# Squares of the first blocks added on VectorE, and the entry's steps in another order

## The chip, the core and the metric

The kernel runs on one core of a Trainium2 chip, as one program. The time is that of one execution on the device, in microseconds (us). The core's engines are TensorE (PE; its weight loads are shown as PEld), VectorE (DVE), ScalarE (ACT), GpSimd (POOL) and SyncE (SP, which here only issues transfers). Each engine works through a queue of its own in order; semaphores tie the queues together.

## What is computed

The reference runs two layers of a streaming encoder over 1024 prompt tokens and 8 x 16 later tokens (together 1152) of width 1024. What matters here is the way into layer 0: each token is divided by the root of its mean square and multiplied by a gain, and one input projection follows, whose columns feed an attention branch and a recurrent branch.

```python
def rms_norm(x, g):
    y = xf * lax.rsqrt(jnp.mean(xf * xf, axis=-1, keepdims=True) + EPS)
    return (y * g.astype(jnp.float32)).astype(x.dtype)
...
h = x @ w_in            # q, k, v, xr (recurrent input), gr (its gate branch)
...
xc, new_buf = causal_conv(xr, conv_buf, conv_w, conv_b)
hs, new_h = rg_lru(xc, h0, wa, ba, wx, bx, lam)
rec = hs * jax.nn.gelu(gr)
```

The recurrence runs h = a h + b along the tokens, with a and b from two sigmoid gates that are products of the convolved input.

## The kernel before, in words

Activations lie transposed: width on the partitions, in 8 tiles of 128 (kt), tokens along the free axis, in three blocks (nb) of 384. Products are made in three passes of a split format: each operand is a high part (hi) and a low part (lo = value - hi), and `three` (L530 to L533) multiplies hi by hi (L531), hi by lo (L532) and lo by hi (L533). So a slab of one 128-column chunk over one block is 8 x 3 = 24 matmuls into one PSUM bank.

The norm's root is left out of the products' operands: a tile is only multiplied by its gain and split (`norm_split`: high part on ScalarE at L527, low part on VectorE at L528), and the root is multiplied in when the product is read from PSUM (`xr_evac`, L679 and L681; for the gate branch L696). The root itself takes these steps for a block:

- `stat` squares a tile (on ScalarE at L478; tile 4 on VectorE at L476) into one of three buffers `tmp`, and adds the square to the block's sum `s`, at L480: on GpSimd, unless `sum_on_dve` is set. At the entry it isn't.
- `stat_tokens`: three small matmuls with a column of ones (L490) give each token's sum; VectorE forms the root `rT` by a chain of small steps (L492, L452 to L457), each of which needs the one before.
- `spread_stat`: three small matmuls (L500) spread `rT` over the partitions; VectorE copies the result to `rstd` (L501).

The entry's order is written by hand in the string `START` (L263 to L265), which a loop (L713) walks. Its words: `w` splits half a weight slab (ScalarE L200, VectorE L201), `nBK` splits tile K of block B, `sBK` squares it and adds, `mCB` makes the slab of recurrent chunk C over block B, `fB` is `stat_tokens`, `FB` `spread_stat`, `eCB` evacuates the slab. Chunks 0 and 1 are made there for all three blocks; chunk 2's slabs follow. The order of issue gives instructions their rank; a scheduler then puts each engine's queue in order from it and from the tiles' dependences.

Behind the entry comes the recurrence stage (chunks c = 0 to 3): convolution (ScalarE L575, VectorE L578), split (L586, L590), gates (products, sigmoids at L613), tanh, exponent and root (L624, L627, L630) on ScalarE, VectorE L636 and L639, GpSimd L633, the scan L649 on VectorE, and then the next chunk's gates. The gate branch's slabs are made beside it, evacuated at L696 and put through GeLU at L700. ScalarE loads a table when it changes between sigmoid, exponent, root and GeLU. After it come attention and the MLPs, which are products for most of the span.

Of the kernel before, what the change touches and what calls it, by code (L numbers as in the profile page):

```python
# [248 lines left out]
class InOrder:  # L249
# [5 lines left out]
    def __getattr__(self, name):  # L255
# [5 lines left out]
ON_DVE = (4,)  # L261
WLOAD = {0: 1, 2: 2}
START = ("n00 w n03 w n01 w s00 n02 w n11 n04 s01 n07 n06 n17 s02 n05 m00 n12 n13 s03 n10 s04 m10 n14 n15 s05 n16 "  # L263
         "n25 s06 s07 m11 f0 n27 m01 s10 n21 s11 s12 n23 s13 n20 s14 s15 s20 s16 n26 n22 F0 s21 n24 m02 e00 m12 s22 s23 "
         "s17 e10 s24 s25 f1 s26 s27 F1 e01 e11 f2 F2 e02 e12")  # L265

LRU_ORDER = [(t[0], int(t[1])) for t in "x2 x2 x2 x3 G0 g0 x3 G1 g0 x3 G2 g0 g1 g1 g1 g2 g2 g2 G3 g3 g3 g3".split()]

# [13 lines left out]
def body(ctx, tc, io):  # L282
# [41 lines left out]
    def bank(tag):  # L324
        bank.n += 1
        p = banks[tag if tag in ("mm", "two") else "ax"].pool
        return p.tile([P, 1024 if tag == "two" else 512], F32, tag=tag, bufs=BANKS[tag], name=f"{tag}{bank.n}")
# [3 lines left out]
    def tmp():  # L331
        tmp.n += 1
        return space["st"].pool.tile([P, NBW], F32, tag="tmp", bufs=3, name=f"tmp{tmp.n}")
# [65 lines left out]
    def pump(act, dve, pl, halves=1):  # L399
        W.pump(halves)  # L400
        bg.pump(act, dve, pl)
# [62 lines left out]
    def stat(nb, kt, src, on_dve=False, sum_on_dve=False):  # L464
        if kt == 0:
            if nb == NB - 1 and "early" in space:
                s = space["early"].pool.tile([P, NBW], F32, tag="xc", bufs=2, name=f"s{stat.n}")
            else:
                s = space["st"].pool.tile([P, NBW], F32, tag="s", bufs=space["sums"], name=f"s{stat.n}")
            stat.n += 1  # L470
            ssum[nb] = s
            sq = s
        else:
            sq = tmp()
        if on_dve:
            nc.vector.tensor_mul(sq, src, src)  # L476
        else:
            nc.scalar.square(sq, src)  # L478
        if kt:
            (nc.vector if sum_on_dve else nc.gpsimd).tensor_add(ssum[nb], ssum[nb], sq)  # L480
# [3 lines left out]
    def stat_tokens(nb, tag="ax"):  # L484

        s = ssum.pop(nb)
        ps = bank(tag)
        n = NBW // P
        for t in range(n):
            nc.tensor.matmul(ps[:, t:t + 1], s[:, t * P:t * P + P], ones, start=True, stop=True)  # L490
        v, w, r = ps[:, 8:8 + n], ps[:, 16:16 + n], rT[:, nb * n:nb * n + n]
        nc.vector.tensor_scalar(v, ps[:, 0:n], 1.0 / D, EPS, OP.mult, OP.add)  # L492
        rsqrt(r, v, w)

    def spread_stat(nb, tag="ax"):
        n = NBW // P
        r = rT[:, nb * n:nb * n + n]
        ps = bank(tag)
        for t in range(n):
            nc.tensor.matmul(ps[:, t * P:t * P + P], r[:, t:t + 1].to_broadcast([P, P]), ident, start=True, stop=True)  # L500
        nc.vector.tensor_copy(rstd[:, nb * NBW:nb * NBW + NBW], ps[:, :NBW])  # L501
# [22 lines left out]
    def norm_split(nb, kt, src, gi):  # L524
        cols = slice(nb * NBW, nb * NBW + NBW)
        g = gt[:, gi, kt:kt + 1]
        nc.scalar.activation(xh[:, kt, cols], src, AF.Copy, scale=g)  # L527
        nc.vector.scalar_tensor_tensor(xl[:, kt, cols], src, g, xh[:, kt, cols].bitcast(F32), OP.mult, OP.subtract)  # L528
# [6 lines left out]
    def slab_bank(key, nb, kts=None, ps=None):  # L535

        h, l = W.get(key)
        cols = slice(nb * NBW, nb * NBW + NBW)
        if ps is None:
            ps = bank("mm")  # L540
        for kt in (kts or range(KT)):
            w = slice(kt * P, kt * P + P)
            three(ps[:, :NBW], h[:, w], l[:, w], xh[:, kt, cols], xl[:, kt, cols], kt == 0, kt == KT - 1)
        return ps
# [126 lines left out]
    def xr_evac(c, nb, ps):  # L671
        if nb == 0:
            t = pads[c] = xp.tile([P, PADW], F32, tag="xa", bufs=4, name=f"pad{c}")
            nc.gpsimd.memset(t[:, 0:3], 0.0)
            nc.gpsimd.tensor_scalar_mul(t[:, S0:].rearrange("p (b w) -> p b w", w=SW)[:, :, 0:3],
                                        lc[:, c, 16:40].rearrange("p (b w) -> p b w", w=3), 1.0)
        t = pads[c]
        n = min(NBW, SEQ - nb * NBW)
        nc.vector.tensor_mul(t[:, 3 + nb * NBW:3 + nb * NBW + n], ps[:, :n], rstd[:, nb * NBW:nb * NBW + n])  # L679
        if n < NBW:  # L680
            nc.vector.tensor_mul(  # L681
                t[:, S0:].rearrange("p (b w) -> p b w", w=SW)[:, :, 3:],
                ps[:, n:NBW].rearrange("p (b w) -> p b w", w=DS),
                rstd[:, SEQ:].rearrange("p (b w) -> p b w", w=DS))
            W.free(("xr", c))
            if c == 0:
                add_conv(0)
# [21 lines left out]
    def x_block(nb, kt):  # L709
        return xs[kt][:, nb * NBW:nb * NBW + NBW]  # L710

    early = {}
    for step in START.split():  # L713
        kind, *n = step[0], *(int(d) for d in step[1:])
        if kind == "w":
            W.split()
        elif kind == "n":
            norm_split(n[0], n[1], x_block(*n), 0)
        elif kind == "s":
            stat(n[0], n[1], x_block(*n), n[1] in ON_DVE)  # L720
        elif kind == "f":
            stat_tokens(n[0])
        elif kind == "F":
            spread_stat(n[0])
        elif kind == "m":
            c, nb = n
            early[c, nb] = slab_bank(("xr", c), nb, ps=bank("mm" if len(early) < 3 else "ax"))
        elif kind == "e":
            xr_evac(*n, early.pop(tuple(n)))
            pump(3200, 2500, 3000, 2)  # L730
# [1044 lines left out]
def build(arrays):  # L1775
    import concourse.bacc as bacc

    nc = bacc.Bacc("TRN2", target_bir_lowering=False, num_devices=1)
    io = {k: nc.dram_tensor(f"in_{k}", v.shape, F32, kind="ExternalInput").ap() for k, v in arrays.items()}
    for k, s in OUTS.items():  # L1780
        io[k] = nc.dram_tensor(f"out_{k}", s, F32, kind="ExternalOutput").ap()
    with tile.TileContext(nc) as tc, ExitStack() as ctx:
        body(ctx, tc, io)
    return nc
# [21 lines left out]
```

## Time and profile before

| | us |
|---|---|
| median of three runs (lowest, highest) | 2216.12 (2213.75, 2217.06) |
| the profiled execution | 2215.67 |
| its span | 2213.9 |
| TensorE busy | 2157.8 |
| VectorE busy | 1614.8 |
| ScalarE busy | 961.8 |
| GpSimd busy | 279.4 |

A timeline's row has the start, the duration, the engine, the line, the instruction, its output and inputs by the program's names, the shape, a count where rows were merged and, in brackets, how long the engine stood idle before it and what released it. Starts can lie closer together than durations are long, since instructions overlap at their ends; the distance of two starts is then the price in a full queue. A row of the waits has the total, the number and the longest. A row of the stretches has, for each engine, the busy time and the number of instructions, then the granted clock of TensorE (1.00 is full), the busy share of the DMA engines and GB/s.

### The profile page before, as it was taken

How to read it: one execution, taken by the hardware profiler on the slowest of the kernel's cores; microseconds unless marked ns; L12 is line 12 of the kernel's file. 1: busy time of each engine (PE TensorE's matmuls, PEld its weight loads, DVE VectorE, ACT ScalarE, POOL GpSimd, SP SyncE). 2: the span in 40 equal slices, each digit the busy share in tenths (PEclk: the TensorE clock that was granted, in tenths of full speed). 3: DMA queues.
4: the chain of work that ended last, by engine and by line, in shares of the span. 5: the costliest groups of instructions: out<-in, count | busy, mean ns of one | idle time of the engine just before them, and what ended most of it. 6: DMA issues, size and time to landing. Idle time of an engine off the chain costs nothing.

```text
span 2213.9 us, 37892 instructions
## 1 busy us (share of the span) xinstructions
PE 2157.8 (97%) x14980; PEld 2114.9 (96%) x14980; DVE 1614.8 (73%) x2810; ACT 961.8 (43%) x1695; POOL 279.4 (13%) x332
## 2 busy tenths in 40 slices
PE   7989999899999999999999999989999999999999
PEld 7978989899999999999988899989999999999999
DVE  8778883798777678777793734269877777877776
ACT  5665663367666642112162123226766665211211
POOL 5147642000000000000050333100000000000000
PEclk9999999999999999999999999999999999999999
DMA  4110043237666777356751013322766667735574
GB/s 156 63 51 9 13 142 103 67 124 278 241 224 243 264 297 291 102 188 248 254 181 50 20 48 109 113 75 94 292 240 231 234 250 308 282 128 205 209 249 149
DMA packets 108003, 377.91 MB, mean 171 GB/s; under 512 B 13473, under 2 KB 24737, under 8 KB 107809
## 3 DMA queue, kind: packets, MB, share of 16 engines
q1 hardware_dynamic: 107680, 375.47, 47.1%
q8 instruction: 118, 1.93, 0.4%
q14 instruction: 61, 0.49, 0.1%
q10 hardware_dynamic: 144, 0.02, 0.0%
HBM read 240.09 MB, written 136.26 MB: 170 GB/s over the span
## 4 chain that ended last, share of the span: by engine, by line
PE 88%; DVE 6%; ACT 2%; issue 2%; DMA 1%; POOL 1%; SPq 0%; ACTq 0%; DVEq 0%; POOLq 0%
PE two L1293 64%; PE mm L533 5%; PE mm L531 5%; PE mm L532 5%; PE mm L257 2%; PE mm L1610 1%; PE mm L1612 1%; PE mm L1611 1%; DVE w L201 1%; PE pv L257 1%; PE tp L257 1%; PE ax L1639 1%; PE qk L257 1%; DVE b L407 0%; DVE x L1492 0%
## 5 line engine op out<-in xcount | busy, mean ns | idle before, releaser
L1293 PE MATMUL two<-b,w 128*128 128x288 f32 x5424 | 728.0, 296 | 12.4 <-DVE x L1137 12.4
L1293 PEld LDWEIGHTS two<-b,w 128*128 128x128 f32 x5424 | 726.7, 189 | 12.9 <-ACT tmp L478 12.9
L1293 PE MATMUL two<-h,w 128*128 128x288 f32 x4704 | 630.6, 295 | 3.2 <-DVE x L1492 1.5
L1293 PEld LDWEIGHTS two<-h,w 128*128 128x128 f32 x4704 | 627.5, 188 | 5.1 <-issue 3.0
L200 ACT CAST w<-raw 128x512 fp32r<-128x512 f32 x542 | 331.2, 620 | 645.9 <-PE two L1293 412.7
L201 DVE TENSOR_TENSOR w<-raw,w 128x512 fp32r<-128x512 f32 x542 | 386.4, 718 | 113.7 <-ACT w L200 111.5
L1492 DVE TENSOR_TENSOR x<-two,x 128x576 f32<-128x576 f32 x448 | 336.3, 754 | 127.9 <-PE two L1293 126.4
L531 PE MATMUL mm<-xn0h,w 128*128 128x384 f32 x372 | 127.8, 343 | 6.3 <-ACT xn0h L527 5.9
L532 PE MATMUL mm<-xn1l,w 128*128 128x384 f32 x372 | 125.6, 338 | 1.1 <-DVE xn1l L528 1.1
L533 PE MATMUL mm<-xn0h,w 128*128 128x384 f32 x372 | 126.3, 340 | 0.0
L532 PE MATMUL mm<-xn0l,w 128*128 128x384 f32 x372 | 126.3, 340 | 0.0
L531 PE MATMUL mm<-xn1h,w 128*128 128x384 f32 x372 | 125.9, 339 | 0.0
L533 PE MATMUL mm<-xn1h,w 128*128 128x384 f32 x372 | 125.7, 338 | 0.0
L1542 POOL TENSOR_TENSOR s<-s,tmp 128x384 f32<-128x384 f32 (+1 forms) x28 | 28.9, 1059 | 730.7 <-ACT tmp L1541 730.6
L1293 PE MATMUL two<-hk,w 128*128 128x288 f32 x672 | 91.2, 295 | 0.0
L407 DVE TENSOR_TENSOR ho<-c_a,ho 128x576 fp32r<-128x576 f32 x78 | 57.2, 753 | 46.1 <-ACT ho L406 46.0
L1293 PEld LDWEIGHTS two<-hk,w 128*128 128x128 f32 x672 | 90.1, 188 | 0.0
L1322 ACT ACTIVATE c_a<-c_a 128x1152 f32<-128x1152 f32 x60 | 70.1, 1168 | 19.3 <-DVE c_a L1404 18.0
L531 PEld LDWEIGHTS mm<-xn0h,w 128*128 128x128 f32 x372 | 71.0, 191 | 7.3 <-ACT xn0h L527 6.6
L407 DVE TENSOR_TENSOR ho<-c_b,ho 128x576 fp32r<-128x576 f32 x96 | 72.3, 753 | 2.5 <-ACT ho L406 2.5
L480 POOL TENSOR_TENSOR s<-s,tmp 128x384 f32<-128x384 f32 x49 | 54.7, 1121 | 148.2 <-ACT tmp L478 146.0
L1137 DVE TENSOR_TENSOR x<-mm,x 128x384 f32<-128x384 f32 x48 | 26.7, 555 | 63.8 <-PE mm L533 63.6
(287 smaller groups left out, 2815.3 us busy)
## 6 DMA issues: line engine op xcount, KB each, us to landing
hidden<-ho SPq DMA_DIRECT2D x196, 576.0 KB, 4.0
h<-hidden SPq DMA_DIRECT2D x196, 576.0 KB, 6.6
raw<-in_w SPq DMA_DIRECT2D x136, 512.0 KB, 4.5
x<-scratch SPq DMA_DIRECT2D x24, 576.0 KB, 7.7
scratch<-x SPq DMA_DIRECT2D x48, 192.0 KB, 1.8
raw<-in_wo SPq DMA_DIRECT2D x16, 512.0 KB, 3.6
xin<-in_xT SPq DMA_DIRECT2D x24, 192.0 KB, 4.2
x<-in_xT SPq DMA_DIRECT2D x8, 576.0 KB, 3.8
```

Of the source, the lines that this page charges most:

```text
L200: nc.scalar.copy(t[:, 0], src)
L201: nc.vector.tensor_sub(t[:, 1], src, t[:, 0].bitcast(F32))
L257: return lambda *a, **k: self.tc.keep_in_program_order(op(*a, **k))
L407: nc.vector.tensor_sub(lo, src, hi.bitcast(F32))
L480: (nc.vector if sum_on_dve else nc.gpsimd).tensor_add(ssum[nb], ssum[nb], sq)
L531: nc.tensor.matmul(ps, wh, ah, start=start, stop=False)
L532: nc.tensor.matmul(ps, wh, al, start=False, stop=False)
L533: nc.tensor.matmul(ps, wl, ah, start=False, stop=stop)
L1293: nc.tensor.matmul(o, w, a[:, c], start=first and k == 0 and i == 0, stop=k == len(pairs) - 1 and i == 2, skip_group_check=True)
L1322: nc.scalar.activation(o, o, AF.Relu) if fn == "relu" else nc.scalar.square(o, o)
L1492: nc.vector.tensor_add(o, both(ps), o)
L1542: nc.gpsimd.tensor_add(o, o, sq)
```

## The change

All additions of squares at the entry go to VectorE, for all three blocks (21 instructions, tiles 1 to 7 of each). And `START` has another order from its 35th word on: block 2's tiles are split before any square of block 1 or 2 is taken, chunk 0's slab over block 2 (`m02`) stands ahead of block 0's spreading (`F0`), and the squares of blocks 1 and 2 come later, block 2's after the whole of block 1's.

```diff
 START = ("n00 w n03 w n01 w s00 n02 w n11 n04 s01 n07 n06 n17 s02 n05 m00 n12 n13 s03 n10 s04 m10 n14 n15 s05 n16 "
-         "n25 s06 s07 m11 f0 n27 m01 s10 n21 s11 s12 n23 s13 n20 s14 s15 s20 s16 n26 n22 F0 s21 n24 m02 e00 m12 s22 s23 "
-         "s17 e10 s24 s25 f1 s26 s27 F1 e01 e11 f2 F2 e02 e12")
+         "n25 s06 s07 m11 f0 n27 m01 n21 n23 n20 n26 n22 n24 m02 F0 s10 s11 e00 s12 m12 s13 s14 s15 s16 e10 s17 f1 "
+         "s20 s21 s22 s23 F1 e01 e11 s24 s25 s26 s27 f2 F2 e02 e12")
...
-            stat(n[0], n[1], x_block(*n), n[1] in ON_DVE)
+            stat(n[0], n[1], x_block(*n), n[1] in ON_DVE, True)
```

What becomes of it in the queues is shown at three places. In the rows, `ax` and `mm` are PSUM banks (the number tells one from another), `w` split weights, `xn0h` and `xn1h` the high parts of tiles 0 to 3 and 4 to 7, `xn0l` and `xn1l` the low parts, `xin` the unsplit tiles, `s` a block's sum.

TensorE around block 0's spreading, before:

```order
L532 MATMUL ax_319<-xn1l_84,w_160 128x384
L533 MATMUL ax_319<-xn1h_83,w_160 128x384
L500 MATMUL ax_376<-ident,rT 128x128 x3
L531 MATMUL ax_386<-xn0h_78,w_155 128x384
L532 MATMUL ax_386<-xn0l_79,w_155 128x384
```

TensorE at the same place now, from the end of chunk 0's slab over block 1 (ax_319):

```order
L533 MATMUL ax_319<-xn1h_83,w_160 128x384
L531 MATMUL ax_356<-xn0h_78,w_155 128x384
L532 MATMUL ax_356<-xn0l_79,w_155 128x384
...
L533 MATMUL ax_356<-xn1h_83,w_160 128x384
L500 MATMUL ax_381<-ident,rT 128x128 x3
L531 MATMUL ax_406<-xn0h_78,w_167 128x384
```

The 24 products of chunk 0 over block 2 (ax_386 before, ax_356 now) stand ahead of the spreading. In the same way, the last spreading has 16 more products ahead of it than before.

VectorE around block 0's root, before:

```order
L492 TENSOR_SCALAR ax_301<-ax_301 128x3
L555 TENSOR_SCALAR small<-lc 128x4
L452 TENSOR_SCALAR ax_301<-ax_301 128x3
L556 TENSOR_TENSOR small<-small,lc 128x4
L528 SCALAR_TENSOR_TENSOR xn1l_84<-xin_102,gt,xn1h_83 128x384
L453 TENSOR_SCALAR rT<-ax_301 128x3
L528 SCALAR_TENSOR_TENSOR xn0l_79<-xin_98,gt,xn0h_78 128x384
L455 SCALAR_TENSOR_TENSOR ax_301<-rT,ax_301 128x3
L476 TENSOR_TENSOR tmp_361<-xin_99 128x384
L456 TENSOR_TENSOR ax_301<-ax_301,rT 128x3
```

VectorE there now:

```order
L528 SCALAR_TENSOR_TENSOR xn1l_84<-xin_100,gt,xn1h_83 128x384
L480 TENSOR_TENSOR s_170<-s_170,tmp_273 128x384
L528 SCALAR_TENSOR_TENSOR xn0l_79<-xin_98,gt,xn0h_78 128x384
L492 TENSOR_SCALAR ax_301<-ax_301 128x3
L528 SCALAR_TENSOR_TENSOR xn1l_84<-xin_102,gt,xn1h_83 128x384
L452 TENSOR_SCALAR ax_301<-ax_301 128x3
L528 SCALAR_TENSOR_TENSOR xn0l_79<-xin_95,gt,xn0h_78 128x384
L453 TENSOR_SCALAR rT<-ax_301 128x3
L528 SCALAR_TENSOR_TENSOR xn1l_84<-xin_101,gt,xn1h_83 128x384
L455 SCALAR_TENSOR_TENSOR ax_301<-rT,ax_301 128x3
```

The last addition of block 0 (L480) is now in this queue, block 2's splits lie between the root's steps, and the preparation of the recurrence's constants (L555, L556) has gone further back.

ScalarE in the recurrence stage, between the second scan and the third, before (`u_1057` is chunk 1's gate branch, `rg` the gates, `h_983` chunk 2's recurrence):

```order
L613 ACT_TABLE_LOAD
L613 ACTIVATE rg_943<-ax_944,lc 128x392
...
L624 ACTIVATE h_983<-rg_943,spc 128x1176
L700 ACT_TABLE_LOAD
L700 ACTIVATE u_1057<-u_1057 128x1152
L627 ACT_TABLE_LOAD
L627 ACTIVATE rg_943<-rg_943,spc 128x1176
```

ScalarE there now:

```order
L700 ACTIVATE u_1057<-u_1057 128x1152
L613 ACT_TABLE_LOAD
L613 ACTIVATE rg_943<-ax_944,lc 128x392
...
L624 ACTIVATE h_983<-rg_943,spc 128x1176
L200 CAST w_1271<-raw_1045 128x512
L627 ACT_TABLE_LOAD
L627 ACTIVATE rg_943<-rg_943,spc 128x1176
```

The GeLU of chunk 1 went ahead of the gates, one table load is gone, and a weight cast stands in the GeLU's place. On VectorE, a gate-branch evacuation (L696) that stood ahead of the third scan stands behind it, and chunk 1's last one stands ahead of the second scan.

## The prediction

> **What bounds the kernel now.** I read the page's busy times first, then TensorE's waits up to 160 us, a table of stretches, and then the timelines of TensorE, VectorE and ScalarE.
>
> ```profile
> PE 2157.8 (97%) x14980; PEld 2114.9 (96%) x14980; DVE 1614.8 (73%) x2810; ACT 961.8 (43%) x1695; POOL 279.4 (13%) x332
> ...
> PE ax L500 <- DVE rT L457: 6.2, 2, 5.0
> ...
> PE mm L532 <- DVE xn1l L528: 1.1, 1, 1.1
> ```
>
> TensorE is the bound over the whole span, so time is to be had only where it stands still or runs slowly. At the entry it stands still for VectorE: 6.2 us in two waits for rT (a block's reciprocal root, which the spreading L500 reads), 1.1 us for a split tile. The stretches show what else that costs (columns: PE, PEld, DVE, ACT, POOL busy, then granted clock).
>
> ```profile
> 26.00:30.00 4.00, 3.55 (x21) 3.23 (x19) 4.00 (x14) 2.11 (x5) 3.44 (x6) 1.00 0.01 2
> 30.00:34.00 4.00, 0.00 (x0) 0.00 (x0) 3.93 (x10) 2.96 (x7) 3.81 (x4) 1.00 0.00 0
> ...
> 52.00:54.00 2.00, 2.00 (x8) 2.00 (x7) 0.96 (x4) 0.00 (x0) 0.00 (x0) 0.50 0.00 0
> ```
>
> From 30 to 34 us TensorE does nothing while VectorE is full. After the second wait for rT the granted clock is 0.50 (52 to 54); after the wait for the split tile it stays 1.00 (26 to 30). The timeline of TensorE gives the prices.
>
> ```profile
> 19.00 0.33 PE L531 MATMUL mm<-xn0h,w 128*128 128x384 f32 x1
> ...
> 21.08 0.33 PE L531 MATMUL mm<-xn1h,w 128*128 128x384 f32 x1
> ...
> 24.55 0.72 PE L490 MATMUL ax<-ones,s 128*128 128x1 f32 x6
> ...
> 34.51 1.38 PE L500 MATMUL ax<-ident,rT 128*128 128x128 f32 x6 [4.96 <-DVE rT L457]
> ...
> 50.28 0.91 PE L500 MATMUL ax<-ident,rT 128*128 128x128 f32 x6 [1.28 <-DVE rT L457]
> 51.02 0.73 PE L490 MATMUL ax<-ones,s 128*128 128x1 f32 x6
> 51.61 0.42 PE L533 MATMUL mm<-xn1h,w 128*128 128x384 f32 x1
> ...
> 52.15 0.52 PE L532 MATMUL mm<-xn1l,w 128*128 128x384 f32 x1
> 52.47 0.52 PE L533 MATMUL mm<-xn1h,w 128*128 128x384 f32 x1
> ...
> 55.34 0.33 PE L533 MATMUL mm<-xn0h,w 128*128 128x384 f32 x1
> ...
> 58.11 0.83 PE L500 MATMUL ax<-ident,rT 128*128 128x128 f32 x6
> 58.70 0.42 PE L531 MATMUL mm<-xn1h,w 128*128 128x384 f32 x1
> ```
>
> Twelve products take 2.08 us (19.00 to 21.08); 0.173 each is the full pace; at the slow one they start 0.32 apart (52.15 to 52.47). A statistic (L490, 51.02 to 51.61) takes 0.59 of TensorE, a spreading (58.11 to 58.70) 0.59.
>
> Why VectorE is late: the same instruction has two durations there.
>
> ```profile
> L528 DVE SCALAR_TENSOR_TENSOR xn0l<-xin,gt,xn0h x12: 602/614/1375, 5.9 to 31.8; 128x384 fp32r<-128x384 f32 x12
> L528 DVE SCALAR_TENSOR_TENSOR xn1l<-xin,gt,xn1h x12: 606/1310/1428, 11.2 to 33.1; 128x384 fp32r<-128x384 f32 x12
> ...
> L480 POOL TENSOR_TENSOR s<-s,tmp 128x384 f32<-128x384 f32 x21 | 25.8, 1231 | 14.9 <-ACT tmp L478 13.0 <-DVE tmp L476 1.0
> ...
> 17.30 0.55 DVE L476 TENSOR_TENSOR tmp<-xin 128x384 f32<-128x384 f32 x1
> 17.77 0.61 DVE L528 SCALAR_TENSOR_TENSOR xn0l<-xin,gt,xn0h 128x384 fp32r<-128x384 f32 x1
> 18.30 5.22 DVE L528 SCALAR_TENSOR_TENSOR xn1l<-xin,gt,xn1h 128x384 fp32r<-128x384 f32 x4
> ...
> 34.31 0.15 DVE L457 SCALAR_TENSOR_TENSOR rT<-ax,rT 128x3 f32<-128x3 f32 x1
> 34.38 2.82 DVE L201 TENSOR_TENSOR w<-raw,w 128x512 fp32r<-128x512 f32 x2
> ```
>
> Alone a low-part split takes 0.61 (0.53 to the next start); while GpSimd's additions run, 1.31. GpSimd has 21 of them, 1.23 each.
>
> **The change part by part.** (1) The 21 additions go from GpSimd to VectorE. No addition of this form is in the trace on VectorE; the nearest row is L476, same shape, 0.47 to the next start, 0.55 long. Below it can't be, since it reads two tiles as L476 does; above, 1.31 if what slows L528 is not GpSimd. I take 0.47: 9.9 us of new work, against 0.70 us given back on each of the 12 splits of the second row and of some 5 more large instructions, 12 us.
>
> (2) The order. I walk VectorE's queue as the new order has it, from the split at 11.24 (not changed before it) to block 0's rT: 20 splits at 0.53 = 10.6; 10 additions and 2 squares at 0.47 = 5.6; two weight splits at 0.7 = 1.4 (the pair at 34.38 takes 1.41 each beside GpSimd; halved, as L528 is without it); 12 steps of the root at 0.07 (34.31 to 34.38, other work between them) = 0.8. The first 15 splits, 7 additions and a square bring it to 22.95, where it waits for the statistic until 23.75: 0.8. Sum 19.2: rT is there at 30.5.
>
> More rows of VectorE: steps of the root that wait for each other start 0.2 apart, and a spread root is copied out 0.87 after its spreading starts (58.11 to 58.98).
>
> ```profile
> 48.57 0.17 DVE L456 TENSOR_TENSOR ax<-ax,rT 128x3 f32<-128x3 f32 x1
> 48.77 0.16 DVE L457 SCALAR_TENSOR_TENSOR rT<-ax,rT 128x3 f32<-128x3 f32 x1
> ...
> 51.22 0.56 DVE L501 COPY rstd<-ax 128x384 f32<-128x384 f32 x1 [1.09 <-PE ax L500]
> ...
> 58.98 0.56 DVE L501 COPY rstd<-ax 128x384 f32<-128x384 f32 x1 [2.56 <-PE ax L500]
> ```
>
> TensorE from 19.00, after block 0's first products: 24 products 4.16, to 23.16; statistic 0.59; block 1's 24 products, to 27.90; block 2's first 24, to 32.06. The splits they need are done by 20.4 (block 1) and 26.9 (block 2), from the same walk, so neither waits. The spreading at 32.06 finds rT waiting 1.5 us: the 4.96 wait goes. Spreading 0.59, 24 products, to 36.81; block 1's sum is ready at about 36.1: its last addition stands behind the copy of the spread root, which starts 0.87 after the spreading, at 32.9, and then the copy, two additions, two evacuations and a weight split at 0.5, 0.47 and 0.7 make 3.1. Statistic, 24 products to 41.55, nine more to 43.11: the second spreading.
>
> Here VectorE's queue has an evacuation that waits for those 24 products ahead of the last three steps of the root, and the root's steps and two later evacuations queue behind it. It ends at about 42.2; three dependent steps at 0.2 make 42.8.
>
> Spare 0.3 us: no wait, or a short one. Spreading and third statistic to 44.28, 15 products to 46.88, 13 to 49.13: the third spreading, whose root is ready at about 48.8 by the same count. So it stands at 49.1 instead of 58.1: **9.0 us** earlier, and it starts the convolutions. Sixteen more products stand ahead of it than before, so TensorE itself is 11.8 us ahead. ScalarE's squares wait for three buffers, which VectorE now frees; by the walk each is free 0.5 us or more before the sum needs it. No DMA is moved past another on SP; the gate and branch weights are fetched earlier, as their buffers come free earlier. GpSimd keeps only small work there.
>
> (3) The recurrence stage behind it has the same instructions in slightly other places.
>
> ```profile
> L200 ACT CAST w<-raw 128x512 fp32r<-128x512 f32 x542 | 331.2, 620 | 645.9 <-PE two L1293 412.7
> ...
> 106.64 1.19 ACT L630 ACTIVATE h<-h 128x1176 f32<-128x1176 f32 x1
> ...
> 109.73 0.56 DVE L696 TENSOR_TENSOR u<-mm,rstd 128x384 f32<-128x384 f32 x1 [4.20 <-PE mm L533]
> ...
> 127.05 1.28 ACT L700 ACT_TABLE_LOAD   x1
> 128.35 1.17 ACT L700 ACTIVATE u<-u 128x1152 f32<-128x1152 f32 x1
> ...
> 139.05 0.56 DVE L696 TENSOR_TENSOR u<-mm,rstd 128x384 f32<-128x384 f32 x1 [1.51 <-PE mm L533]
> ...
> 140.20 2.60 DVE L649 TENSOR_TENSOR_SCAN h<-rg,rg 128x1176 f32<-128x1176 f32 x1
> ...
> 158.00 0.79 PE L257 MATMUL mm<-w,xn1h 128*128 128x512 f32 x1 [2.58 <-ACT w L200]
> ```
>
> At 109.73 a wait of VectorE for products ends, and the step behind this evacuation goes on about 110.2, while the root that it needs (L630) was ready at 107.83: with TensorE further ahead than VectorE's chain, 2.3 us go. Chunk 1's GeLU and its table load, 2.45 us, leave the chain between the second gates and the third scan and go ahead of the gates, where ScalarE waits; a weight cast (0.62) takes their place: 1.8 net. The evacuation at 139.05 goes behind the scan: the scan could start at 137.5 instead of 140.2, 2.7. Together 6.8, and TensorE's wait at 158.00 would shrink so that it can follow. Each of these three needs products in time that the trace can't show. I count two thirds, 4.5.
>
> **Sum:** 9.0 + 4.5 = 13.5 us. The profiled execution took 2215.67 us, 1.8 above its span and 0.45 below the median of the runs (2216.12): 2215.7 - 13.5 = **2202**. From the attention on, all instructions stand in the same order, so the rest shifts.
>
> [...] The trace has 0.50 clock from 52 to 54 after an idle stretch of only 1.28 us followed by 1.33 us of statistics and spreading, and 1.00 after 1.1 us idle and one statistic at 24.55. In the new order 1.18 us of such small work stand together without idle time: less than either, so I charge no spell. [...]
>
> **Rivals.** *The entry alone.* The recurrence stage gives nothing more, since its products come just as late: 2215.7 - 9.0 = 2206.7. For it: every one of its terms is a wait in another engine's queue; against it: the table load and its GeLU leave ScalarE's chain whatever TensorE does. Chance 0.27.
>
> *All of it.* 15.8, and the wait at 158.00 (2.58) goes whole, with the clock that it costs: 15.8 + 2.6 = 18.4 at most, 2197 to 2200. Chance 0.09.
>
> *Eaten in the recurrence stage.* GpSimd's L633 comes to lie on more of VectorE's splits of the convolved tiles:
>
> ```profile
> 103.23 1.37 DVE L590 TENSOR_TENSOR xcl<-y,xch 128x1176 fp32r<-128x1176 f32 x1
> ...
> 125.89 2.95 DVE L590 TENSOR_TENSOR xcl<-y,xch 128x1176 fp32r<-128x1176 f32 x1 [1.24 <-ACT xch L586]
> ```
>
> 1.6 each, two more of the four; with one new slow spell of twelve products (51.61 to 55.34; 12 x 0.15 = 1.8) and a scan put back by the evacuation now ahead of it (0.5), 5.5 of the 9.0 go: 2212. Within 0.2%, which (4.4 us) is about what a measurement of this kernel can tell from no change. Chance 0.09. *It doesn't do what it says:* VectorE reaches the roots no earlier and the two waits stay, 2216; the walk's spare 1.5 us at the first speaks against it. Chance 0.02.
>
> *Slower.* What stretches L528 to 1.31 is not GpSimd. Then the additions cost VectorE 9.9 us and give nothing back; its idle time around the last two spreadings (1.09 and 2.56, rows 51.22 and 58.98) covers 3.7, and the products start 6.2 later: 2221.9. It decides if less than 6.2 of the 12 us come back, that is if L528, 1.31 beside GpSimd, stays above about 0.95. The short splits before 11.2 us, with GpSimd idle, speak against it. Chance 0.04.
>
> **How the numbers follow.** Forecast (2200 to 2205) 0.49. The range runs from all of it, 2197, to the entry alone less a spell of 1.8 and 0.6 for additions at 0.55 with dependent steps, 2209. Faster: 0.49 + 0.27 + 0.09 = 0.85; same: 0.09 + 0.02 = 0.11; slower 0.04.
>
> **What would show it.** Right: L528 near 0.6 throughout; L480 on VectorE near 0.55; no TensorE wait for rT over 0.5; third spreading near 49; granted clock 1.00 from 19 to 60; the third scan, 140.20 before, 9 to 16 us earlier. Wrong: L528 still above 1; a wait at the second spreading for the evacuation ahead of the root; a third scan less than 9 us earlier; or a lead at 60 us that is lost by 165.

## The result, and the profile after

| | before | after |
|---|---|---|
| median (lowest, highest), us | 2215.03 (2213.75, 2217.06) | 2202.37 (2201.94, 2203.06) |
| the profiled execution | 2215.67 | 2201.94 |
| its span | 2213.9 | 2200.2 |

Four runs each. The ratio is 0.9944, with a 95% interval from 0.9932 to 0.9957: 12.7 us less by the medians, 13.7 by the spans. The forecast was 2202.

The page's busy times of the changed kernel, first part:

```profile
PE 2154.8 (98%) x14980; PEld 2112.9 (96%) x14980; DVE 1606.5 (73%) x2831; ACT 961.4 (44%) x1694; POOL 257.9 (12%) x311
```

VectorE has 21 instructions more and is busy 8.3 us less (1614.8 before): moving work onto it unloaded it. GpSimd has 21 less. TensorE's waits up to 160 us, in the changed kernel (total, times, longest):

```profile
PE mm L531 <- ACT xn0h L527: 6.4, 2, 6.2
PE ax L531 <- ACT rg L613: 3.4, 2, 2.8
PE mm L257 <- DVE w L201: 2.7, 1, 2.7
PE ax L532 <- DVE xcl L590: 1.3, 1, 1.3
```

The waits for rT (6.2) and for the split tile (1.1) are gone; the first row is the wait for the input, there before. The same three stretches as shown of before:

```profile
26.00:30.00 4.00, 4.00 (x25) 4.00 (x24) 3.97 (x14) 2.18 (x5) 0.00 (x0) 1.00 0.04 6
30.00:34.00 4.00, 4.00 (x27) 4.00 (x26) 3.25 (x10) 1.57 (x3) 0.00 (x0) 1.00 0.16 60
52.00:54.00 2.00, 2.00 (x13) 2.00 (x13) 1.97 (x4) 2.00 (x3) 1.69 (x4) 1.00 0.13 27
```

From 30 to 34 us, where TensorE did nothing, it is full; GpSimd, full before, does nothing; the clock is 1.00 in all three. Read in steps of 1 us, the clock before was 0.50 from about 35 to 39 us too, behind the first wait for rT, and from 52 to 56; now it is 1.00 from 19 to 60. TensorE's timeline, its statistics (L490) and spreadings (L500):

```profile
23.11 0.72 PE L490 MATMUL ax<-ones,s 128*128 128x1 f32 x6
...
32.11 0.83 PE L500 MATMUL ax<-ident,rT 128*128 128x128 f32 x6
...
36.97 0.72 PE L490 MATMUL ax<-ones,s 128*128 128x1 f32 x6
...
43.36 0.83 PE L500 MATMUL ax<-ident,rT 128*128 128x128 f32 x6
44.03 0.73 PE L490 MATMUL ax<-ones,s 128*128 128x1 f32 x6
...
49.56 0.83 PE L500 MATMUL ax<-ident,rT 128*128 128x128 f32 x6
```

None has a wait in brackets. The third spreading starts at 49.56 instead of 58.11, 8.55 earlier. VectorE's splits, all of them:

```profile
L528 DVE SCALAR_TENSOR_TENSOR xn0l<-xin,gt,xn0h x12: 606/608/619, 6.2 to 25.8; 128x384 fp32r<-128x384 f32 x12
L528 DVE SCALAR_TENSOR_TENSOR xn1l<-xin,gt,xn1h x12: 603/607/619, 11.5 to 26.4; 128x384 fp32r<-128x384 f32 x12
```

Shortest, median and longest are one number now, 0.61; before, the second row's median was 1.31. The additions, in the groups by line:

```profile
L480 DVE TENSOR_TENSOR s<-s,tmp 128x384 f32<-128x384 f32 x21 | 11.5, 552 | 0.1
```

0.55 each, 0.47 to the next start.

Further on the lead (start before less start after) is read off equal places: 8.55 at the third spreading, 11.0 at the first scan (91.47 and 80.50), 12.2 at the second (117.83, 105.61), 14.9 at the third (140.20, 125.34), 14.85 at the attention's table load (178.38, 163.53), 14.84 at 312 us. It ends at 13.7. VectorE's rows of the changed kernel in the recurrence stage:

```profile
97.57 0.56 DVE L696 TENSOR_TENSOR u<-mm,rstd 128x384 f32<-128x384 f32 x1 [3.01 <-PE mm L533]
98.04 1.37 DVE L636 SCALAR_TENSOR_TENSOR h<-rg,h 128x1176 f32<-128x1176 f32 x1
...
110.66 3.54 DVE L578 SCALAR_TENSOR_TENSOR y<-pad,lc,y 128x1176 f32<-128x1176 f32 x1
...
125.34 2.61 DVE L649 TENSOR_TENSOR_SCAN h<-rg,rg 128x1176 f32<-128x1176 f32 x1
127.86 0.53 DVE L696 TENSOR_TENSOR u<-mm,rstd 128x384 f32<-128x384 f32 x1
```

The evacuation that stood ahead of the third scan (139.05 before) stands behind it. At 97.57 VectorE still waits 3.01 for products ahead of L636. A convolution step takes 3.54 beside GpSimd's L703 and L705, against 1.43 alone.

Of the 1.1 us lost later, 0.67 is one row of TensorE that before doesn't have:

```profile
1115.22 3.46 PE L1293 MATMUL two<-h,w 128*128 128x288 f32 x24 [0.67 <-DVE x L1492]
```

VectorE came late there after a weight addition that met GpSimd: in the changed kernel

```profile
1102.28 1.55 DVE L185 TENSOR_TENSOR raw<-raw,raw 128x512 f32<-128x512 f32 x1 [0.68 <-DMA raw<-in_w]
```

against 0.69 for the same row of before, at 1116.55. Before, GpSimd's work began 0.12 us after that row and met the split behind it instead (1.57 long); over both rows VectorE loses 0.46 more in the changed kernel. Where the remaining 0.4 to 0.5 us of the 1.1 go is not shown here.

### The profile page after: what moved, and what is told of

Same layout as the page of the kernel before. It is cut to its first block, busy times and chain, and to the rows that moved or that the text cites. A ratio compares the mean times of both kernels' runs of the same rounds, so it can differ in the third digit from the quotient of the medians.

```text
span 2200.2 us, 37883 instructions
## 1 busy us (share of the span) xinstructions
PE 2154.8 (98%) x14980; PEld 2112.9 (96%) x14980; DVE 1606.5 (73%) x2831; ACT 961.4 (44%) x1694; POOL 257.9 (12%) x311
## 4 chain that ended last, share of the span: by engine, by line
PE 90%; DVE 6%; ACT 2%; issue 1%; POOL 1%; DMA 1%; SPq 0%; ACTq 0%; DVEq 0%; POOLq 0%
PE two L1293 64%; PE mm L531 5%; PE mm L533 5%; PE mm L532 5%; PE mm L257 2%; PE mm L1610 1%; PE mm L1611 1%; PE mm L1612 1%; DVE w L201 1%; PE pv L257 1%; PE tp L257 1%; PE ax L1639 1%; PE qk L257 1%; DVE b L407 0%; DVE x L1492 0%
## 5 line engine op out<-in xcount | busy, mean ns | idle before, releaser
L201 DVE TENSOR_TENSOR w<-raw,w 128x512 fp32r<-128x512 f32 x542 | 382.2, 710 | 107.6 <-ACT w L200 105.6
L532 PEld LDWEIGHTS mm<-xn0l,w 128*128 128x128 f32 x372 | 70.9, 191 | 0.5 <-DVE xn0l L528 0.5
```

Of the source, the lines that this page charges most:

```text
L201: nc.vector.tensor_sub(t[:, 1], src, t[:, 0].bitcast(F32))
L532: nc.tensor.matmul(ps, wh, al, start=False, stop=False)
```

## The experiments

The theory: GpSimd's additions stretch VectorE's instructions; with them gone the new order hides the first root behind block 2's products; and the recurrence stage gets shorter since TensorE is further ahead. Rivals: the order alone did it; the additions alone did it; what stretches VectorE isn't GpSimd. The ratios are to the kernel before on the same chip; "F2" is the start of the third spreading, "scan 1" and "scan 3" those of L649, "load" that of the attention's table load.

| kernel | median, us (runs) | ratio [95%] | F2 | scan 1 | scan 3 | load | span |
|---|---|---|---|---|---|---|---|
| before | 2215.03 (4) | 1 | 58.11 | 91.47 | 140.20 | 178.38 | 2213.9 |
| after | 2202.37 (4) | 0.9944 [0.9932, 0.9957] | 49.56 | 80.50 | 125.34 | 163.53 | 2200.2 |
| a5_after_again | 2201.04 (5) | 0.9935 [0.9922, 0.9948] | 49.08 | 80.04 | 124.90 | 163.52 | 2200.9 |
| e1_adds_only | 2202.71 (4) | 0.9940 [0.9925, 0.9955] | 50.66 | 82.28 | 125.93 | 165.44 | 2199.0 |
| e1b_adds_only | 2203.23 (5) | 0.9944 [0.9931, 0.9956] | 49.59 | 81.20 | 124.86 | 164.46 | 2200.6 |
| e2_order_only | 2215.01 (10) | 0.9997 [0.9988, 1.0006] | 59.16 | 93.17 | 138.35 | 176.54 | 2213.4 |
| e3_ghost_adds | 2215.60 (10) | 0.9995 [0.9985, 1.0005] | 64.83 | 96.24 | 140.55 | 178.75 | 2213.9 |
| e3b_ghost_copies | 2207.01 (1) | | 53.62 | 84.99 | 129.31 | 167.48 | 2205.3 |
| e4_spread_first | 2204.35 (10) | 0.9954 [0.9937, 0.9970] | 50.61 | 83.34 | 125.96 | 165.72 | 2202.4 |
| e5_block0_adds | 2213.49 (10) | 0.9993 [0.9984, 1.0002] | 56.34 | 89.93 | 135.36 | 173.54 | 2209.3 |
| c1_gate_product_dve | 2199.62 (4) | 0.9924 [0.9908, 0.9940] | 48.79 | 79.45 | 122.85 | 161.02 | 2200.0 |
| c1b_gate_product | 2199.46 (5) | 0.9932 [0.9919, 0.9946] | 48.66 | 79.32 | 122.71 | 161.32 | 2197.3 |
| c2_gelu_product_dve | 2200.89 (4) | 0.9935 [0.9921, 0.9949] | 49.86 | 80.83 | 124.93 | 163.90 | 2199.5 |
| c3_both_products | 2200.39 (5) | 0.9933 [0.9921, 0.9946] | 49.93 | 80.58 | 123.45 | 162.81 | 2199.8 |

F2 moves by about half a microsecond between executions of one kernel (49.56 and 49.08); the difference is there at the first statistic already (23.11 and 22.54).

### The additions alone

```diff
 (on the kernel before)
-            stat(n[0], n[1], x_block(*n), n[1] in ON_DVE)
+            stat(n[0], n[1], x_block(*n), n[1] in ON_DVE, True)
```

> Only the 21 additions on VectorE, in the order of before. By the prediction's prices VectorE's queue to block 0's rT is 19 splits at 0.53, 13 additions and 2 squares at 0.49, the statistic's 0.8 and the root's 0.8: rT at about 30.5, as in the changed kernel, but TensorE reaches the spreading at 27.9, 24 products earlier, so the wait of 4.96 shrinks to 2.5 and does not go. Theory (GpSimd's additions stretch VectorE, the order covers the rest): third spreading near 49 to 51, against 58.1 before; 16 products fewer ahead of it than in the changed kernel; time 2205 to 2209. Rival (the order alone made the gain): within 3 us of before, 2212 to 2215. Rival (the additions alone made it): 2202, as the changed kernel.

Measured: 2202.71, the whole gain, as the last rival had it, and F2 at 50.66 as the theory had it. TensorE's timeline:

```profile
30.19 1.37 PE L500 MATMUL ax<-ident,rT 128*128 128x128 f32 x6 [2.57 <-DVE rT L457]
...
44.47 0.83 PE L500 MATMUL ax<-ident,rT 128*128 128x128 f32 x6
...
50.66 0.83 PE L500 MATMUL ax<-ident,rT 128*128 128x128 f32 x6
```

So the entry went by the walk: a wait of 2.57 (2.5 expected) stays, 7.45 us are won. What the theory had wrong is the rest of the way: the lead grows to 14.3 at the third scan without the new `START`. There too no evacuation (L696) stands right ahead of that scan any more; one comes behind it, at 129.04. So taking the additions off GpSimd was enough to change VectorE's order in the recurrence stage.

> The additions alone once more, in more rounds, against the changed kernel's 2201.0 to 2202.4. If the order gives what the lead at 165 us shows (1.9 us), 2203 to 2204; if it gives nothing, 2201 to 2202.5.

Measured: 2203.23. TensorE's timeline in this profile:

```profile
30.67 0.91 PE L500 MATMUL ax<-ident,rT 128*128 128x128 f32 x6 [2.57 <-DVE rT L457]
...
49.59 0.83 PE L500 MATMUL ax<-ident,rT 128*128 128x128 f32 x6
```

The wait is the same, and the third spreading is 8.52 us earlier than before, as in the changed kernel (8.55). The first profile had a spell of 3.4 us at half clock behind the wait, which costs 1.7, and this one has none; the last section shows both. What stays of the wait of 2.57 is that TensorE has made 16 products (2.8 us) fewer by the third spreading than in the changed kernel.

Over nine runs each, the median is 2202.89 for the additions alone and 2201.97 for the changed kernel. The order's share beside the additions is therefore about 0.9 us, with intervals that overlap and runs from different chips; at the table load it is 0.9 in the profile without the spell and 1.9 in the one with it. Nothing and 2 us are both still possible.

### The order alone

```diff
 (on the changed kernel)
-            stat(n[0], n[1], x_block(*n), n[1] in ON_DVE, True)
+            stat(n[0], n[1], x_block(*n), n[1] in ON_DVE)
```

> Only the new order, the additions on GpSimd as before. Theory: L528 stays at about 1.3 wherever GpSimd adds; block 0's seven additions (8.6 us of GpSimd) stretch some 7 splits by 0.7, 4.6 us, about what the ten additions cost VectorE in the changed kernel, so rT(0) is again near 31 and hidden behind block 2's products; but the 14 additions of blocks 1 and 2 take GpSimd 17.2 us from about 28, so the third statistic waits until about 45 to 46 and the third spreading comes 1 to 3 us later than in the changed kernel (49.6): 2203 to 2207. Rival (the additions alone made the gain): 2212 to 2215.

Measured: 2215.01, no change; the expectation failed, and the rival's 2212 to 2215 holds. Block 2's products do cover part of the first root: its wait is 1.78 instead of 4.96. But the second spreading waits 4.85 for its root. TensorE's waits up to 165 us, the row for rT, and VectorE's timeline ahead of the second of them:

```profile
PE ax L500 <- DVE rT L457: 6.6, 2, 4.9
```

```profile
38.52 0.56 DVE L476 TENSOR_TENSOR tmp<-xin 128x384 f32<-128x384 f32 x1 [2.88 <-POOL s L480]
...
42.39 0.86 DVE L564 TENSOR_TENSOR small<-small 128x4 f32<-128x4 f32 x1
43.29 0.17 DVE L565 TENSOR_SCALAR small<-small 128x4 f32<-128x4 f32 x1
...
45.67 0.16 DVE L564 TENSOR_TENSOR small<-small 128x4 f32<-128x4 f32 x1
...
47.15 0.16 DVE L492 TENSOR_SCALAR ax<-ax 128x3 f32<-128x3 f32 x1
```

VectorE first stands still 2.88 for a buffer that GpSimd holds, then the products among the small preparing steps (L564) take 0.84 to 0.86 each until GpSimd ends its additions at 45.4, and 0.16 after; the root's first step (L492) comes at 47.15. I had counted GpSimd's own time and not these two. The wait of the one root went to the other. And the third spreading has as many products ahead of it as before here, not 16 more.

### GpSimd kept busy with work that nobody reads

```diff
 (on the changed kernel)
+    ghost = lr("rg", "ghost", [P, NBW])
+    nc.gpsimd.memset(ghost, 1.0)
...
             norm_split(n[0], n[1], x_block(*n), 0)
+            if n[0] or n[1] in (2, 4, 5, 6, 7):
+                lo = xl[:, n[1], n[0] * NBW:n[0] * NBW + NBW].bitcast(F32)
+                nc.gpsimd.tensor_add(ghost, ghost, lo)
```

> The changed kernel with 21 additions of the same size put on GpSimd again, on a scratch tile that nobody reads; they follow the low-part splits. Theory (GpSimd's access stretches VectorE): L528 goes to about 1.3 for some 20 splits, 14 us; rT(0) 8 to 14 us later, of which the products cover 1.6; 2209 to 2214. Rival (the stretching came from something else): L528 stays at 0.61 and the time at 2202.

Measured: 2215.60, a little above what the theory had; the whole gain is gone, though no instruction of the changed kernel reads a result of these. The groups by line from 10 to 60 us, of VectorE:

```profile
L480 DVE TENSOR_TENSOR s<-s,tmp 128x384 f32<-128x384 f32 x21 | 16.8, 806 | 0.1
L528 DVE SCALAR_TENSOR_TENSOR xn1l<-xin,gt,xn1h 128x384 fp32r<-128x384 f32 x12 | 10.3, 872 | 0.0
...
L201 DVE TENSOR_TENSOR w<-raw,w 128x512 fp32r<-128x512 f32 x5 | 6.5, 1306 | 0.0
```

Each line is a mean over instructions that met GpSimd (L480 and L528 up to 1.37) and some that didn't; the changed kernel has 0.55, 0.61 and 0.68. This shows the cause: GpSimd's running stretches VectorE's instructions. The first root is there at 43.6, 13 us later than in the changed kernel, within the 8 to 14 expected. The third spreading:

```profile
64.83 0.83 PE L500 MATMUL ax<-ident,rT 128*128 128x128 f32 x6
```

It is a stronger dose than what the change took away. VectorE now has the 21 additions and GpSimd's company besides, and the third spreading comes 6.7 us later than in the kernel before (58.11); from there to the table load this kernel takes 113.9 us, as the changed one (114.0), and the kernel before 120.3. That the time equals that of before is a coincidence of these two.

For the second kernel the addition is a copy, `nc.gpsimd.tensor_scalar_mul(ghost, lo, 1.0)`.

> As the kernel with 21 scratch additions on GpSimd, but each a copy of the same tile (one operand read instead of two). If every GpSimd instruction that reads SBUF holds VectorE up, L528 goes to about 1.1 to 1.3 where they run and the time to 2210 to 2216; if only those with two operands do, L528 stays at 0.61 and the time at 2201 to 2203.

Measured, in a single run: 2207.01, between the two expectations. The same groups of its VectorE, and below them GpSimd's:

```profile
L480 DVE TENSOR_TENSOR s<-s,tmp 128x384 f32<-128x384 f32 x21 | 13.6, 649 | 0.1
L528 DVE SCALAR_TENSOR_TENSOR xn1l<-xin,gt,xn1h 128x384 fp32r<-128x384 f32 x12 | 7.7, 657 | 0.0
```

```profile
L723 POOL TENSOR_SCALAR ghost<-xn1l 128x384 f32<-128x384 f32 x12 | 15.1, 1259 | 0.9
```

The copies last as long as the additions (1.26 against 1.22), but of VectorE's instructions beside them one takes 0.85 (L480, 19.71 to 23.63 us) and the next 0.61 (L528), where beside the additions each takes 1.35 to 1.37: 0.25 to 0.30 more per copy instead of 0.75 to 0.8 per addition. So neither alternative holds as it was put: a GpSimd instruction that reads one operand does hold VectorE up, but for a third of the time.

### The spreading ahead of the products

```diff
 (on the changed kernel)
-... n22 n24 m02 F0 s10 s11 e00 ...
+... n22 n24 F0 m02 s10 s11 e00 ...
```

> The changed kernel with block 0's spreading ahead of block 2's 24 products. Theory: TensorE waits 2.0 to 2.6 us for rT (from 27.9 to about 30.5), and the clock may be at 0.50 for some products after it (0 to 1.8); nothing behind it gives that back: 2204.5 to 2207. Rival (slack later in the entry or the recurrence stage takes it up): 2202 to 2203.

Measured: 2204.35, 2.4 more than the changed kernel's 2201.97. TensorE's timeline:

```profile
30.12 1.61 PE L500 MATMUL ax<-ident,rT 128*128 128x128 f32 x6 [2.64 <-DVE rT L457]
...
50.61 0.83 PE L500 MATMUL ax<-ident,rT 128*128 128x128 f32 x6
```

The wait of 2.64 is there, and the granted clock is 0.50 from 31 to 33 us, 0.56 and 0.73 in the microseconds around it, a spell of 3.4. F2 comes 1.05 later, with 16 products fewer made by then (2.8): TensorE is 3.8 us back, and 2.2 (table load) to 2.4 (medians) of that reach the end, just under what was expected. At half pace the spell costs 1.7 of it in this profile; the additions alone, with the same wait and in one profile without a spell, are 0.9 behind. So the cover is worth some 1 to 2 us.

### Block 0's additions alone

```diff
 (on the changed kernel)
-            stat(n[0], n[1], x_block(*n), n[1] in ON_DVE, True)
+            stat(n[0], n[1], x_block(*n), n[1] in ON_DVE, n[0] == 0)
```

> The changed kernel with only block 0's seven additions on VectorE; the 14 of blocks 1 and 2 on GpSimd. Theory: rT(0) stays hidden (no wait at the first spreading), but GpSimd needs 1.2 each and holds VectorE up again, small steps too (128x4 steps took 0.86 beside it against 0.16 alone in the order-only kernel), so the second and third roots come late: a wait of 2 to 5 us at the second spreading, third spreading at 52 to 57, time 2205 to 2212. Rival (only what stands ahead of block 0's root counts): third spreading at 50, 2202.

Measured: 2213.49, near nothing of the gain, and more than the 2205 to 2212 expected. TensorE's timeline:

```profile
33.62 0.91 PE L500 MATMUL ax<-ident,rT 128*128 128x128 f32 x6 [1.95 <-DVE small L556]
...
41.81 0.41 PE L531 MATMUL mm<-xn0h,w 128*128 128x384 f32 x1 [2.54 <-DVE pad L679]
...
48.46 0.91 PE L500 MATMUL ax<-ident,rT 128*128 128x128 f32 x6 [3.46 <-DVE rT L457]
```

Even the first root comes late, which the theory had as hidden: three of VectorE's last splits (1.30 to 1.39 each, between 23.9 and 28.5 us) and a weight split ahead of the root's last steps (1.42) lie beside additions that GpSimd kept. Block 0's additions alone are not enough; two blocks of three were not tried.

### GpSimd's products of the recurrence stage

```diff
 (on the changed kernel; c1: the first pair, c2: the other two, c3: all)
-            nc.gpsimd.tensor_mul(gi, gi, y)
+            nc.vector.tensor_mul(gi, gi, y)
...
-        nc.gpsimd.tensor_mul(h, h, u[:, :SEQ])
+        nc.vector.tensor_mul(h, h, u[:, :SEQ])
...
-        nc.gpsimd.tensor_mul(hs, hs, u[:, SEQ:].rearrange("p (b w) -> p b w", w=DS))
+        nc.vector.tensor_mul(hs, hs, u[:, SEQ:].rearrange("p (b w) -> p b w", w=DS))
```

> The changed kernel itself again, beside the others of this call, so that differences of 1 to 2 us can be read: 2202 to 2203. If the new order is worth what the leads at 165 us show (14.9 with it, 12.9 with the additions alone), it stands 1 to 2 us below the kernel with the additions alone; if a short spell at half clock near 1150 us comes and goes from run to run, single profiles differ by up to 1.8 for that alone.

> The changed kernel with the recurrence's product of gate and convolved tile (L633) on VectorE instead of GpSimd: 4 x 1.38 more on VectorE, and the splits and convolution steps that lay beside it (2.27 and 3.21 x2 for 0.68 each, some 5 us in all) back to their own time. Theory (the two engines block each other, and here ScalarE's chain covers VectorE's lateness): about nothing, 2201 to 2203. Rival (the same swap as at the entry pays here too): 2197 to 2200.

> The changed kernel with the products of scan and GeLU (L703, L705) on VectorE instead of GpSimd: 4 x about 1.5 more on VectorE; the convolution steps L578 at 101 and 111 us back from 3.6 to 1.43 each. The one at 111 us holds the cast that the third gates need (TensorE waits 1.67 more there than before). Theory: the third scan 1 to 2 us earlier, 2200 to 2202. Rival (VectorE has no room, the scans move back by the 1.5 each): 2203 to 2206.

> The changed kernel with L633 on VectorE once more, in more rounds: at 165 us it stood 2.5 us ahead of the changed kernel, of which 0.8 came from an earlier start of the input. If the rest is its own, 2199 to 2200.5; if it was chance, 2201 to 2202.5.

> L633, L703 and L705 on VectorE, so that GpSimd keeps only small copies up to 145 us. L703 alone moved the third scan by nothing beyond the noise of the start, L633 alone by 1.7: together 2199 to 2200.5. Rival (VectorE is now full, 11 us more work in this stage): 2202 to 2205.

Measured: the changed kernel again 2201.04 (2202 to 2203 expected); c1 2199.62 and 2199.46; c2 2200.89; c3 2200.39. c1's groups by line from 60 to 165 us, of VectorE, and the same of the changed kernel:

```profile
L578 DVE SCALAR_TENSOR_TENSOR y<-pad,lc,y 128x1176 f32<-128x1176 f32 x8 | 13.6, 1702 | 0.4 <-ACT y L575 0.4
L201 DVE TENSOR_TENSOR w<-raw,w 128x512 fp32r<-128x512 f32 x19 | 12.5, 680 | 0.7 <-ACT w L200 0.7
...
L633 DVE TENSOR_TENSOR rg<-rg,y 128x1176 f32<-128x1176 f32 x4 | 5.5, 1380 | 6.1 <-ACT rg L613 6.1
```

```profile
L578 DVE SCALAR_TENSOR_TENSOR y<-pad,lc,y 128x1176 f32<-128x1176 f32 x9 | 17.2, 1915 | 0.2 <-ACT y L575 0.2
L201 DVE TENSOR_TENSOR w<-raw,w 128x512 fp32r<-128x512 f32 x19 | 16.0, 865 | 0.7 <-ACT w L200 0.7
```

The four products cost VectorE 5.5; L201 gives back 3.5 (19 x 0.185) and L578 1.7 (8 x 0.21): nearly even, as at the entry. From the third spreading to the table load c1 takes 112.2 and 112.7 us, the changed kernel 114.0 and 114.4: 1.3 to 2.2 less. Over nine runs each, c1's median is 2199.46 and the changed kernel's 2201.97, 2.5 apart, but the runs come from different chips (on the chip that has both, 1.4 apart), and the intervals overlap. So the swap seems to pay here too, by 1 to 2.5 us, nearer to the rival than to "about nothing"; these runs don't settle it.

c2 lies in the range expected, but its third scan comes no earlier (124.93), so its reason failed. L578 is back at 1.43 and the wait for the cast of the third gates is gone. But chunk 1's GeLU and its table load stand between the third gates and the third scan again, from 113.40 on, as in the kernel before. c3, with both swaps, isn't below c1.

## Why the prediction was right

**Additions, step 1: right.** 0.55 each on VectorE at a pitch of 0.47, all splits at 0.61. From 10 to 60 us the splits give back 8.1 (21.1 to 13.0), five weight splits 2.5 and three squares 1.1, together 11.7, where 12 were forecast. GpSimd as the cause of the 1.31, argued there, is shown by the scratch additions; the rival "slower" falls.

**The walk, step 2: right, to 0.45 us.** rT(0) at 30.63 (30.5 forecast), spreadings at 32.11, 43.36 and 49.56 (32.06, 43.11, 49.13). 9.0 forecast, 8.55 measured. But the walk treated both halves of the change as one, and said nothing on what each is worth: the additions alone win 7.45 of it in a profile with a spell at half clock and 8.52 in one without, the order alone loses 1.05. The cover that the walk describes is there (no wait at 32.11), but it is worth only some 1 to 2 us: the additions alone, without it, end 0.9 behind.

**The recurrence stage, step 3: the sum near, its parts not.** 4.5 was forecast on top of 9.0, and from F2 to the table load 6.3 came. Term by term, from the leads: (a), L636 behind an evacuation: 2.3 forecast, 1.2 measured, since that evacuation still waits 3.01 for products. (b), the GeLU out of ScalarE's chain: 1.8 forecast, 0.2 measured; the time was taken back by L578 at 3.54 beside L703 and L705, which kept the third gates waiting. (c), L696 behind the third scan: 2.7 forecast, 2.5 measured. And 2.4 between F2 and the first scan was not in the sum at all. The 16 products that stand ahead of F2 explain it in part at most: the additions alone, without them, have 1.7 of it in both profiles. TensorE's wait at 158.00 was to shrink, so that it could follow; it didn't, a wait of 2.75 for VectorE's weight split stands there now, at 146.40.

The discount was given because products must come in time. For (a) that held: the 3.01 is such a wait. For the stage as a whole it isn't TensorE's lead that decides. From the first to the third scan before takes 48.7 us and the changed kernel 44.8. Kernels whose entry is no faster (order alone, scratch additions) take 45.2 and 44.3, and the additions alone, whose entry has no 16 products more, 43.7. That points to the other order of instructions in this stage. Which of its changes does it was not separated: with the additions alone the GeLU stays in ScalarE's chain, and the time is as short.

**"The rest shifts": nearly, and the sum with some luck.** 14.84 of lead at 312 us, 13.7 at the end. The entry gave 0.45 less than forecast, the recurrence stage 1.8 more, and the rest of the span took 1.1 back, which the forecast had at nothing. That 2202 was met to within 0.4 us is owed in part to these errors, which cancelled.

**The clock: right for this entry.** No spell stands between 19 and 60 us, as the sum had it. The prediction's reason for that, less small work in a row (1.18 us) than at the two places read, was an estimate from those two; no run shows that this decides. The prediction named the spell from 52 and not the one from 35 to 39, which went too; its walk had full pace at both places. That the same wait had a spell behind it in one profile and none in another is shown below.

**The rivals.** Eaten in the recurrence stage (2212) and no effect (2216) fell with the waits gone and 14.85 of lead at the table load. The entry alone (2206.7) fell, as the recurrence stage gave its part; all of it (2197 to 2200) fell, as (a) and (b) gave less than their whole. Taking L703 off GpSimd doesn't bring it (c2, 2200.89).

## What to carry to other kernels

Read an instruction's duration per occurrence: two values for one shape (0.61 and 1.31) can mean that another engine is in its way, and taking that engine's work over can make the receiving engine less busy. Test a reason by putting the suspected cost back as work nobody reads, and read what comes of it at the place it should act on, since the total can agree by chance; and test an order without what came along with it. A change that moves instructions to another engine can also move the order far behind it, so the lead is to be followed from place to place up to the end.

## What the runs showed of the hardware

**What VectorE loses beside GpSimd depends on GpSimd's instruction, not on its length.** Additions of two operands, 1.22 long, cost a 128x384 instruction of VectorE 0.75 to 0.8 each (1.35 to 1.37 instead of 0.61 and 0.55); copies of one operand, 1.26 long, cost 0.25 to 0.30 each (0.85), and the instruction after it nothing (0.61). A 128x4 product went from 0.16 to 0.86 beside the additions. So VectorE loses less than GpSimd's instruction lasts, in both cases; how much of GpSimd's own duration is waiting, no run here shows.

**The half clock came behind a wait in one profile and not behind the same wait in another; its spells lasted 3.4, 6.8 or 10.2 us.** The kernel with the additions alone was profiled twice, with the same wait of 2.57 us ahead of the first spreading. First profile, then the second (the granted clock is the third column from the right):

```profile
28.00:30.00 2.00, 0.00 (x0) 0.00 (x0) 1.97 (x9) 1.87 (x5) 0.00 (x0) 1.00 0.00 0
31.00:33.00 2.00, 2.00 (x9) 2.00 (x9) 1.44 (x4) 0.07 (x1) 0.00 (x0) 0.50 0.00 0
```

```profile
28.00:30.00 2.00, 0.10 (x1) 0.00 (x0) 1.94 (x8) 2.00 (x5) 0.00 (x0) 1.00 0.00 0
31.00:33.00 2.00, 2.00 (x15) 2.00 (x14) 1.91 (x4) 0.52 (x1) 0.00 (x0) 1.00 0.00 0
```

9 products or 15 in the same two microseconds. Later, near 1150, the ten profiles read there have the same short stall of 1.2 us (1.5 with the order alone), and nine of them one of 0.94 before it. The stretch behind them in the changed kernel, with the additions alone (first profile), and in c1 (first profile):

```profile
1150.00:1154.00 4.00, 4.00 (x14) 3.25 (x14) 4.00 (x27) 0.00 (x0) 1.09 (x1) 0.57 0.04 8
```

```profile
1152.00:1156.00 4.00, 4.00 (x20) 3.31 (x20) 4.00 (x27) 0.00 (x0) 1.09 (x1) 1.00 0.03 4
```

```profile
1147.00:1153.00 6.00, 6.00 (x20) 5.13 (x20) 5.99 (x33) 0.00 (x0) 1.42 (x1) 0.50 0.22 51
```

One spell, none, and one of twice the length. Read in steps of one microsecond, these spells last 3.4 us or 6.8 us, and one of the kernel with the scratch additions, from 27.8 us on, 10.2; at half pace that is 0, 1.7 or 3.4 us for one and the same stall near 1150. That is as much as the order's whole share, and may be part of why runs of one kernel lie up to 5 us apart. Stalls of 1.2 us (near 1150, the changed kernel) and 1.28 us (ahead of the second spreading, the kernel before), with small products behind them, were followed by it; the one of 1.2 with the additions alone, and stalls of 1.78 and 1.95 us (order alone, block 0 alone), weren't. What sets it off, these runs don't show.

What stays open: whether the new order is worth anything beside the additions (0.9 us by the medians), and which change of order in the recurrence stage shortens it, and why the additions bring it about.
